# A copy of four norm factors to all partitions by GpSimd, placed behind the issue of the transfer that gathers the factors' row

## The chip, the cores and the metric

One core of one Trainium2 chip. The metric is the device time of one execution in microseconds (us), lower is better; the median of three runs is compared.

## What is computed

Two encoder layers over 512 tokens of width 1024, in float32. Each layer normalises x by its root mean square, sends it through one wide input projection, runs three attention branches (multi-head latent attention, a neighbourhood attention on a grid, a sliding-window attention), gates and sums them, projects and adds to x; then a second norm, an up projection of 2 x 2816 columns, a convolution of width 3 along the tokens, a gated GELU and a down projection. The part that matters here:

```python
def rmsnorm(x, g):
    y = xf * lax.rsqrt(jnp.mean(xf * xf, axis=-1, keepdims=True) + EPS)
    return (y * g.astype(jnp.float32)).astype(x.dtype)
...
h = rmsnorm(x, norm1_g[l])
...
q = (rmsnorm(c_q, g_qa) @ w_uq)
kv = (rmsnorm(c_kv, g_kva) @ w_ukv)
...
h = rmsnorm(x, norm2_g[l])
```

So each token has a factor 1/sqrt(mean square) for each of these norms, and each factor scales one column of the activations.

## The kernel before, in words

Activations lie transposed: 128 channels on the partitions, 512 tokens along a row, so x is eight tiles of 128x512. Every float32 matrix and activation is split into a high and a low part (`split`, lines 145 to 152: ScalarE casts the high part, VectorE subtracts to get the low part), and every product is three matmuls (lines 162 to 164). Weights come through a ring of three raw tiles, filled by transfers on SyncE's queue (line 114), and are split into `whi` and `wlo`, three pairs deep (lines 120 to 131).

The norm is applied after the product. `rs_tokens` (line 184) turns the sums of squares with four TensorE transposes, reduces them on VectorE (L193) and makes the factors on GpSimd: `ms` (L195, L196), then `rt` (L198, L200), a 128x4 tile that holds token 128j+p in row p, column j. `rs_spread` (line 203) brings the 512 factors to every partition: a transfer on GpSimd's queue writes `rt` as one row of one partition (`row`, L207), and GpSimd's partition_broadcast copies that row to all 128 partitions (L208), into `rb` or `rbk`. It runs six times, three times a layer:

- in `do_lat` (line 404), where the first norm's `rb` is made; the lines behind it, 416 and 417, make `r1` from `rt` with two GpSimd instructions, which `rs_q` and `rs_k` need at L195 and L200. In layer 0 `do_lat4` (lines 423 and 424) then issues two parameter transfers on GpSimd's queue, each behind a small GpSimd copy that holds it back until `rt` is there;
- in `do_rb_k` (line 470), where the kv latent's `rbk` is made, which `do_kn` (line 494) multiplies into the keys (`ev`, L155);
- at the up projection (line 869), where the second norm's `rb` is made, which `conv` (line 877) multiplies into the products (`u`, L155).

Readers of `rb` in the attention stage are the key rotation (`do_kr`, line 450) and the gates (line 687). The values V take `rtk` itself as a scale on ScalarE (line 467, `ynh`).

**Order.** TensorE and SyncE run in program order, written by hand in the lists of `schedule`. VectorE, ScalarE and GpSimd are ordered by the framework's planner when the program is built: it plays the program through with modelled times, and when an engine is free in that play, the engine takes, of the instructions whose inputs are there, the one that stands first in the program. Weight splits are put ahead in this ranking (`high_priority(offset=PRIO)`, line 129). The chip then runs each engine's list in exactly that order, and an instruction whose input is late holds up all that is listed behind it. GpSimd's library loads are put into the finished lists afterwards, wherever an instruction needs other library code than the one before: in the profile they are pairs of MODIFY_POOL_CONFIG. The broadcast needs one library, the tensor_tensor and tensor_scalar instructions of GpSimd (L195 to L200, L416, L417) another.

Of the kernel before, what the change touches and what calls it, by code (L numbers as in the profile page):

```python
# [10 lines left out]
F32 = mybir.dt.float32  # L11
# [6 lines left out]
P = 128  # L18
# [40 lines left out]
class Trunk:  # L59
# [143 lines left out]
    def rs_spread(self, rt, rb):  # L203


        row = self.const.tile([P, S], F32, tag="sq0", name="row")
        self.nc.gpsimd.dma_start(row[0:1, :], rt[:])  # L207
        self.nc.gpsimd.partition_broadcast(rb[:].rearrange("q (j p) -> q j p", p=P),  # L208
                                           row[0:1, :].rearrange("q (p j) -> q j p", p=P))

# [882 lines left out]
```

## Time and profile before

| | |
|---|---|
| median of three runs | 1702.35 us (1701.78 to 1702.51) |
| the profiled execution | 1702.94 us, its span 1701.2 us |
| TensorE busy | 1694.5 us, 100% of the span |
| VectorE, ScalarE, GpSimd busy | 1145.2, 867.4 and 53.1 us |
| broadcasts on GpSimd | 6, of 1.2 us each |

Times in the rows below are microseconds from the span's start; the second column is an instruction's length; in brackets stands how long its engine sat idle before it and what ended that ("issue": nothing that the profile shows as work, such as a library load). POOL is GpSimd, DVE is VectorE, ACT is ScalarE, PE is TensorE, PEld its weight loads. L numbers are lines of the kernel. What lies outside the span is 1.7 us.

### The profile page before, as it was taken

To read this page: it belongs to the slowest core of one execution; us is meant where nothing else is said; L and a number is where in the kernel's file an instruction comes from. 1 tells how busy PE (TensorE), PEld (TensorE's weight loads), DVE (VectorE), ACT (ScalarE), POOL (GpSimd) and SP (SyncE) were. 2 spreads that over 40 slices of the span, in tenths; PEclk is the share of its full clock that TensorE was granted. 3 is DMA by queue.
4 is the path that set the end of the run, shared out by engine and by line. 5 is a ranking of instruction groups with operands and counts; after the bars stand their busy time and mean duration, and the time that the engine had idled before them with its cause. 6 is when DMAs were issued, how large, how long until landed. Compare 5 with 4: busy or idle time off the path is not lost.

```text
span 1701.2 us, 21123 instructions
## 1 busy us (share of the span) xinstructions
PE 1694.5 (100%) x7924; PEld 1416.0 (83%) x7924; DVE 1145.2 (67%) x1872; ACT 867.4 (51%) x1504; POOL 53.1 (3%) x107
## 2 busy tenths in 40 slices
PE   9999999999999999999999999999999999999998
PEld 8888888888888888888888888888888888888887
DVE  7767885887558777734367678768766587777234
ACT  7665555775435444433256656557744444444232
POOL 1100000000000000000011100000000000000000
PEclk9999999999999999999999999999999999999999
DMA  5223233222324333323233232432223333333231
GB/s 178 80 83 84 82 93 87 75 69 75 106 81 118 99 100 99 96 87 103 81 96 81 81 84 69 107 85 69 63 81 107 98 112 99 94 93 98 87 105 69
DMA packets 289398, 155.38 MB, mean 91 GB/s; under 512 B 9008, under 2 KB 285248, under 8 KB 289296
## 3 DMA queue, kind: packets, MB, share of 16 engines
q1 hardware_dynamic: 286752, 148.92, 30.7%
q0 software_dynamic: 2256, 4.83, 1.0%
q8 instruction: 62, 1.02, 0.3%
q14 instruction: 40, 0.33, 0.1%
q10 hardware_dynamic: 288, 0.29, 0.0%
HBM read 151.89 MB, written 2.10 MB: 91 GB/s over the span
## 4 chain that ended last, share of the span: by engine, by line
PE 96%; DVE 0%; DMA 0%; issue 0%; ACT 0%; ACTq 0%
PE ps_d L162 21%; PE ps_d L164 21%; PE ps_d L163 21%; PE ps_g L164 7%; PE ps_g L162 7%; PE ps_g L163 7%; PE ps_tp L816 1%; PE ps_po L672 1%; PE ps_tp L526 1%; PE ps_tp L657 1%; PE ps_s L786 1%; PE ps_s L785 1%; PE ps_po L831 1%; PE ps_po L830 1%; PE ps_s L639 0%; PE ps_s L638 0%
## 5 line engine op out<-in xcount | busy, mean ns | idle before, releaser
L148 ACT CAST whi<-raw 128x1024 fp32r<-128x1024 f32 (+4 forms) x339 | 301.4, 889 | 572.6 <-PE ps_d L163 344.2
L162 PE MATMUL ps_d<-hh,whi 128*128 128x512 f32 x1328 | 518.6, 391 | 0.0
L164 PE MATMUL ps_d<-hh,wlo 128*128 128x512 f32 x1328 | 517.2, 389 | 0.0
L163 PE MATMUL ps_d<-hl,whi 128*128 128x512 f32 x1328 | 517.1, 389 | 0.0
L149 DVE TENSOR_TENSOR wlo<-raw,whi 128x1024 fp32r<-128x1024 f32 (+4 forms) x337 | 344.7, 1023 | 173.9 <-ACT whi L148 173.1
L164 PEld LDWEIGHTS ps_d<-hh,wlo 128*128 128x128 f32 x1328 | 249.2, 188 | 52.7 <-DVE wlo L149 0.5
L162 PEld LDWEIGHTS ps_d<-hh,whi 128*128 128x128 f32 x1328 | 249.3, 188 | 50.7 <-DVE rot L155 0.5
L163 PEld LDWEIGHTS ps_d<-hl,whi 128*128 128x128 f32 x1328 | 249.4, 188 | 50.1
L162 PE MATMUL ps_g<-ff,whi 128*128 128x512 f32 x334 | 129.9, 389 | 0.0
L163 PE MATMUL ps_g<-ff,whi 128*128 128x512 f32 x334 | 129.9, 389 | 0.0
L164 PE MATMUL ps_g<-ff,wlo 128*128 128x512 f32 x334 | 129.9, 389 | 0.0
L155 DVE TENSOR_TENSOR u<-ps_d,rb 128x512 f32<-128x512 f32 x80 | 55.3, 691 | 63.1 <-PE ps_d L164 63.1
L155 DVE TENSOR_TENSOR gz<-ps_d,rb 128x512 f32<-128x512 f32 x48 | 33.1, 690 | 82.0 <-PE ps_d L164 81.9
L880 ACT ACTIVATE c<-u,par 128x512 f32<-128x512 f32 x88 | 71.7, 815 | 16.4 <-DVE u L155 16.2
L163 PEld LDWEIGHTS ps_g<-ff,whi 128*128 128x128 f32 x334 | 62.7, 188 | 13.1
L162 PEld LDWEIGHTS ps_g<-ff,whi 128*128 128x128 f32 x334 | 62.7, 188 | 13.0
L164 PEld LDWEIGHTS ps_g<-ff,wlo 128*128 128x128 f32 x334 | 62.7, 188 | 13.0
L149 DVE TENSOR_TENSOR pl<-ps_tp,ph 128x512 fp32r<-128x512 f32 x104 | 68.4, 682 | 3.2 <-ACT ph L148 2.9
L886 ACT ACTIVATE c<-c 128x512 f32<-128x512 f32 x44 | 27.8, 632 | 80.5 <-DVE c L882 80.5
L882 DVE SCALAR_TENSOR_TENSOR c<-u,par,c 128x511 f32<-128x511 f32 x88 | 66.0, 750 | 2.8
L881 DVE SCALAR_TENSOR_TENSOR c<-u,par,c 128x511 f32<-128x511 f32 x88 | 65.5, 745 | 0.6 <-ACT c L880 0.6
L148 ACT CAST ph<-ps_tp 128x512 fp32r<-128x512 f32 x104 | 56.9, 585 | 3.6 <-PE ps_tp L526 2.8
(283 smaller groups left out, 2580.9 us busy)
## 6 DMA issues: line engine op xcount, KB each, us to landing
raw<-in_w_in_dram SPq DMA_DIRECT2D x86, 512.0 KB, 4.0
raw<-in_w_up_dram SPq DMA_DIRECT2D x80, 512.0 KB, 3.8
raw<-in_w_down_dram SPq DMA_DIRECT2D x32, 512.0 KB, 4.2
raw<-in_w_down_dram SPq DMA_DIRECT2D x16, 384.0 KB, 3.5
raw<-in_w_in_dram SPq DMA_DIRECT2D x18, 256.0 KB, 2.9
raw<-in_w_br_mla_dram SPq DMA_DIRECT2D x16, 256.0 KB, 2.7
raw<-in_w_br_na_dram SPq DMA_DIRECT2D x16, 256.0 KB, 2.7
raw<-in_w_br_gqa_dram SPq DMA_DIRECT2D x16, 256.0 KB, 2.7
```

What stands on the lines that cost most here:

```text
L148: nc.scalar.copy(hi, src)
L149: nc.vector.tensor_sub(lo, src, r32(hi))
L155: self.nc.vector.tensor_tensor(out, a, b, ALU.mult)
L162: mm(ps, sh, mh, start=first and k == 0, stop=False)
L163: mm(ps, sh, ml, start=False, stop=False)
L164: mm(ps, sl, mh, start=False, stop=last and k == n - 1)
L526: self.nc.tensor.transpose(tp[:, b * P:(b + 1) * P], self.pts[h, b][:, kc * P:(kc + 1) * P], self.idf)
L657: self.nc.tensor.transpose(tp[:, i * P:(i + 1) * P], self.pts["n", h, bp][:, i // 2, (i % 2) * P:(i % 2) * P + P], self.idf)
L880: nc.scalar.activation(c, u, AF.Identity, bias=pr[:, PC_CB + fi:PC_CB + fi + 1], scale=cw[:, 1:2])
L881: nc.vector.scalar_tensor_tensor(c[:, 1:], u[:, :S - 1], cw[:, 0:1], c[:, 1:], ALU.mult, ALU.add)
L882: nc.vector.scalar_tensor_tensor(c[:, :S - 1], u[:, 1:], cw[:, 2:3], c[:, :S - 1], ALU.mult, ALU.add)
L886: nc.scalar.activation(c, c, AF.Gelu_apprx_tanh)
```

## The change

`rs_spread` gets a tile `few` of 128x4 and, between the issue of the transfer and the broadcast of the row, a second partition_broadcast, which copies the first row of `rt` (four factors) to all partitions. Nothing reads `few`.

```diff
     def rs_spread(self, rt, rb):
         row = self.const.tile([P, S], F32, tag="sq0", name="row")
         self.nc.gpsimd.dma_start(row[0:1, :], rt[:])
+        few = self.small.tile([P, 4], F32, tag="few", name="few", bufs=1)
+        self.nc.gpsimd.partition_broadcast(few[:], rt[0:1, :])
         self.nc.gpsimd.partition_broadcast(rb[:].rearrange("q (j p) -> q j p", p=P),
                                            row[0:1, :].rearrange("q (p j) -> q j p", p=P))
```

## Rows read from the trace of the kernel before

**Rows 1.** The page, busy time of each engine: us (share), instructions.
```profile
PE 1694.5 (100%) x7924; PEld 1416.0 (83%) x7924; DVE 1145.2 (67%) x1872; ACT 867.4 (51%) x1504; POOL 53.1 (3%) x107
```
**Rows 2.** TensorE's timeline, the longest wait between two matmuls after the start.
```profile
68.69 0.39 PE L510 MATMUL ps_s<-kr,qr 128*128 128x512 f32 x1
69.34 0.50 PE L506 MATMUL ps_s<-kn,qn 128*128 128x512 f32 x1 [0.27 <-DVE pt L513]
```
**Rows 3.** Waits of TensorE's weight loads: us in total, times, longest.
```profile
PEld ps_d L164 <- DVE wlo L149: 0.5, 2, 0.3
```
**Rows 4.** Lines L208 and L207: library loads of the broadcasts; landing of the row.
```profile
L208 POOLq MODIFY_POOL_CONFIG  x12: 11/37/37, 30.4 to 1340.8; - x12
...
DMA to landing us min/median/max: 2.0/2.4/4.3
```
**Rows 5.** GpSimd's timeline, the first norm of layer 0 to its keys.
```profile
9.60 0.30 POOL masks.py:199 TENSOR_SCALAR_AFFINE_SELECT idf<-idf 128x128 f32<-128x128 f32 x1 [8.67 <-issue]
...
26.08 0.86 POOL L207 DMA_DIRECT2D row<-rt  x1 [0.31 <-POOL rt L198]
26.98 0.21 POOL L416 TENSOR_TENSOR r<-rt 128x4 f32<-128x4 f32 x1
...
37.16 1.25 POOL L208 PARTITION_BROADCAST rb<-row  x1 [6.99 <-issue]
45.21 0.87 POOL L195 TENSOR_TENSOR ms<-ms,r 128x4 f32<-128x4 f32 x1 [6.80 <-DVE acc L181]
...
47.60 0.57 POOL L200 TENSOR_TENSOR rt<-rt,r 128x4 f32<-128x4 f32 x1
51.07 0.58 POOL L195 TENSOR_TENSOR ms<-ms,r 128x4 f32<-128x4 f32 x1 [2.89 <-DVE ms L193]
...
53.97 0.43 POOL L200 TENSOR_TENSOR rt<-rt 128x4 f32<-128x4 f32 x1
54.69 0.74 POOL L207 DMA_DIRECT2D row<-rt  x1 [0.30 <-POOL rt L200]
61.41 1.21 POOL L208 PARTITION_BROADCAST rbk<-row  x1 [5.98 <-issue]
```
**Rows 6.** GpSimd's timeline, the first norm of layer 1.
```profile
857.43 0.74 POOL L207 DMA_DIRECT2D row<-rt  x1 [0.30 <-POOL rt L198]
...
858.65 0.26 POOL L417 TENSOR_SCALAR r<-rt 128x4 f32<-128x4 f32 x1
865.54 1.24 POOL L208 PARTITION_BROADCAST rb<-row  x1 [6.63 <-issue]
884.15 0.20 POOL L195 TENSOR_TENSOR ms<-ms,r 128x4 f32<-128x4 f32 x1 [17.38 <-DVE ms L193]
...
893.00 0.58 POOL L195 TENSOR_TENSOR ms<-ms,r 128x4 f32<-128x4 f32 x1 [6.13 <-DVE ms L193]
```
**Rows 7.** VectorE's timeline, the first reader of layer 1's rb.
```profile
888.64 0.68 DVE L155 TENSOR_TENSOR ev<-ev,rb 64x512 f32<-64x512 f32 x1
```
**Rows 8.** GpSimd's timeline, the broadcast for the up projection of layer 1.
```profile
1347.43 1.22 POOL L208 PARTITION_BROADCAST rb<-row  x1 [6.94 <-issue]
```
**Rows 9.** ScalarE and VectorE at the same place.
```profile
1344.93 0.62 ACT L148 CAST whi<-raw 128x512 fp32r<-128x512 f32 x1 [2.10 <-PE ps_g L163]
...
1348.68 0.69 DVE L155 TENSOR_TENSOR u<-ps_g,rb 128x512 f32<-128x512 f32 x1 [5.12 <-POOL rb L208]
...
1349.29 0.68 DVE L149 TENSOR_TENSOR wlo<-raw,whi 128x512 fp32r<-128x512 f32 x1
```
**Rows 10.** VectorE and ScalarE in layer 0: first readers of rb, rtk and rbk.
```profile
46.71 0.68 DVE L155 TENSOR_TENSOR ev<-ev,rb 64x512 f32<-64x512 f32 x1
...
54.43 0.69 ACT L151 ACTIVATE ynh<-ps_d,rt 128x512 fp32r<-128x512 f32 x1 [1.54 <-POOL rt L200]
...
62.65 0.69 DVE L155 TENSOR_TENSOR ev<-ps_d,rbk 128x512 f32<-128x512 f32 x1 [2.91 <-POOL rbk L208]
```
**Rows 11.** The windows view: stretch, length, then busy us (instructions) of PE, PEld, DVE, ACT, POOL; granted clock.
```profile
62.00:75.00 13.00, 12.73 (x57) 10.21 (x56) 9.37 (x22) 9.33 (x19) 0.62 (x1) 1.00 0.27 76
```

## The prediction

> **What bounds the kernel now.** First the page: TensorE is busy 1694.5 of 1701.2 us [rows 1], so a change on GpSimd, busy for 53.1 us, can only act through a wait of TensorE. Second, TensorE's timeline and waits, for how much it waits at all after the start. The longest gap is at 69.34, where a score product follows its predecessor's start (68.69) by 0.65 us instead of the 0.23 us of a steady stream, 0.42 us lost [rows 2]; the only other wait that hangs on this change is that of two products for a low weight part, 0.5 us together for the loads, about 0.1 us each for the products [rows 3]. So hardly 0.6 us can be won here. Third, GpSimd's timeline around the six broadcasts. Before each of them GpSimd sits idle for 5.98 to 6.99 us though the row has landed 2.0 to 4.3 us after its issue [rows 4 to 6, 8]: what fills the gap is the library load, a pair of MODIFY_POOL_CONFIG [rows 4] that starts behind the instruction before it, not behind the row's landing. The reader should see two things. The load already runs beside the transfer. And what comes after the load of layer 0 is tight: VectorE waits 2.91 us for `rbk` and ScalarE 1.54 us for the factors `rtk` [rows 10].
>
> **What the planner knows.** At the up projection VectorE's list has `u` ahead of a weight split `wlo`; `wlo` had its input at 1345.55 (ScalarE's cast ends), while `u` had to wait for `rb` until 1348.68 [rows 9]. Weight splits rank higher, so in the planner's play `u` must have been startable before that cast was done, some 3 us earlier than on the chip: the planner's GpSimd has no library load in it. Without the load `rb` would be there at about 1343.0: the issue ends at 1340.49 (6.94 ahead of the broadcast), the row lands 2.0 us after the start of a 0.74 us issue, so 1.3 later, and the broadcast takes 1.22 [rows 4 to 6, 8]. That fits.
>
> **The change part by part.** Nothing is removed or moved in the program's text. Added are six broadcasts of four elements, no transfer, no reader.
>
> *What one costs by itself.* The trace has no broadcast of four elements. From above it costs what one of 512 costs, 1.25 us [rows 5]; from below the 0.2 us of a four-element instruction on GpSimd [rows 5, 6]; it might even cost less than nothing if it takes a share of a first call's time off the broadcast behind it, but that one would have to get shorter by more than the new one is long, and I exclude that. I take 0.3 us, near the four-element rows, since the work is four elements.
>
> *Where it goes.* `few` needs `rt` alone, which is there before the transfer is issued, and it stands ahead of `r1` in the program; the row's broadcast has to wait for the landing. So in the play GpSimd takes the issue, then `few`, and then, while the row is still under way (landing 2.0 us after an issue of 0.74 us leaves 1.3 us, and `few` takes 0.3), the two `r1` instructions, as it takes them before the row's broadcast now [rows 5, 6]. At the two first norms the list then reads: issue, `few`, `r1`, `r1`, (in layer 0 the parameter copies and transfers), broadcast, `rs_q`. The library changes at each step: to the broadcast's, back, to the broadcast's, back. Two loads become four. At the other four places (`rbk` and the up projection of both layers) only the row's broadcast follows, in the same library: no further load.
>
> *Prices of a load.* To the broadcast's library 6.99 us at this place [rows 5], 5.98 to 6.94 elsewhere [rows 5, 6, 8]. Back: the only tight row is 6.80 us, but its end may be VectorE's, which is named as releaser [rows 5], so it is an upper bound there; from below I take the shortest load of the other kind, 5.98; from above the very first load of the kernel, 8.67 [rows 5]. I take 6.5.
>
> *Layer 0, step by step* [rows 5]. The issue ends at 26.94. Load 6.99: `few` at 33.9, done 34.2. Load back 6.5: `r1` at 40.7. From there to the end of the parameter issues as now, 26.98 to 30.17 (37.16 less 6.99), 3.2 us: 43.9. Load 6.99 and 1.25 for the row: `rb` at 52.2, 13.8 later than 38.41. Load back 6.5: `rs_q` starts at 58.7, lasts 45.21 to 48.17, 3.0: 61.6. `rs_k` (51.07 to 54.40, 3.3) follows at once, as its inputs are there: `rtk` at 65.0, 10.6 later than 54.40. Then 0.3 and the issue 0.74, load 5.98, `few` 0.3, broadcast 1.21: `rbk` at 73.5, **10.9 us later** than 62.62. What queues behind: VectorE stands at 46.71 until `rb` is there, 5.5 us, which holds the next weight splits; ScalarE stands at 54.43 until `rtk` is there, with the casts of the next weights behind it, so TensorE runs out of weights at about 62; VectorE then stands at 62.65 for `rbk` [rows 10]. The last of these decides, since the score products need the keys, and the present gap at 69.34 [rows 2] hangs on the same chain: all of the 10.9 us shows on TensorE. With 5.98 for every load the term is 7.9; with 8.67 for the loads back and 1.25 for `few`, 17.1.
>
> The Trainium skill (GPSIMD Engine Reference, Instruction dispatch) has a freshly loaded library cost about 6 us, measured as 5.95. By that price for all five loads the term would be an estimated 7.7 in place of 10.9, and the time about 1712. This trace's rows are longer in four of six cases (the two places not shown read 6.92 and 5.98), so I stay with them.
>
> *Layer 1, first norm* [rows 6, 7]. The issue ends at 858.17; 6.63, 0.3, 6.5, 0.7 (`r1`), 6.63 and 1.24 put `rb` at 880.2, before its first reader at 888.64. Load back: `rs_q` at 886.7 instead of 884.15, done before `rs_k` at 893.00. Cover: 8 us for `rb`, and the long way to the first scores for `rs_q`. Cost nothing.
>
> *The other three places.* `rbk` of layer 1 and both `rb` of the up projection come 0.3 us later. VectorE waits for each already [rows 9], and the two low weight parts of [rows 3] are listed behind `u`: 0.6 us for both up projections. For `rbk` of layer 1 TensorE has no gap now, so between 0 and 0.3; I take 0.1. With 1.25 for `few` these would be 3.7.
>
> *TensorE's clock.* It is at 1.00, the 2.4 GHz level, throughout [rows 11], and no wait here is long enough to show what one of 8 us does. If it falls to the lower level the products that follow take twice 0.23 us. From below 0; from above the six products of the second head's keys and the twenty of the first scores, 5.9 us. I take the six, 1.4 us: they are the first behind the last wait, and what ran slowly before that wait is paid in it. The Trainium skill (TensorE: Matmul & The Clock Gate, the clock gate) has a long idle TensorE drop to 1.2 GHz and come back after some work; no run here shows it.
>
> **The sum.** 10.9 + 0.6 + 0.1 + 1.4 = 13.0 us. On the profiled execution 1702.94 + 13.0 = 1715.9; that execution stood 0.6 us above the median, so 1715.3 against 1702.35. A measurement of this kernel can tell about 0.2%, 3.4 us, from no change.
>
> **The rivals.** *One: the two broadcasts stay together at every place* (the planner holds `r1` back, or puts `few` behind it). The place is the first norm, the price the two loads, and what decides is whether in the play the row lands before `r1` is taken. Then no load is added, the row's broadcast comes 0.3 us later, and only the small terms are left: 0.6 + 0.1 + 0.3 for layer 0's `rbk`, 1703.4; with 1.25 for `few` 1707. For it: where nothing else is ready, GpSimd goes straight on to the broadcast [rows 8]. Against it: `r1` is taken ahead of the row in both layers now. Chance 0.19. *Two: the change does nothing*, because nobody reads `few` and it is dropped, or because it lies wholly inside a load's shadow: 1702.35. Chance 0.04. *Three: it helps.* If `few` and row together run ahead of the parameter issues, layer 0's `rb` comes at 35.4 instead of 38.4, but its reader starts at 46.71 [rows 10]; if a second call is much shorter than 1.2 us, the waits of VectorE shrink. All waits together give 0.6 us: 1701.7, within the measurement. Chance 0.02 with a gain that could be told.
>
> **How the numbers follow.** The forecast, loads doubled at the first norms, 0.75: 1715.3, with its own range 1710.5 (loads at 5.98, clock unmoved, little for `few`) to 1719 (a quarter of the upper extras, which are 6.2, 3.0 and 4.5 us). The range must reach down to the first rival to leave out no more than 2 in 10: 1702.6 to 1719. Slower by over 0.2%: 0.75 and a small part of the first rival, 0.78. Same: 0.20. Faster: 0.02.
>
> **What would show it.** Right: GpSimd's timeline with four idle stretches of 6 to 7 us between 27 and 59, `rb` at about 52, `rbk` at about 73, TensorE waiting some 8 us near 62 and 3 us near 72, MODIFY_POOL_CONFIG in more pairs, a granted clock under 1.00 near 75. Layer 1 shows the same loads and no gap on TensorE. Wrong: `few` and the row's broadcast side by side at 27 to 38, and TensorE's timeline unchanged.

## The result and the profile after

The changed kernel takes 1710.44 us (median of five runs, 1710.27 to 1711.02) against 1702.35 us: the ratio is 1.0046, with a 95% interval from 1.0035 to 1.0057, so it is slower by 8.1 us. One of the five runs of the kernel before took 7416 us, which does not move its median. Its profiled execution took 1710.27 us with a span of 1708.4 us, 7.2 us more than the one of before. The difference between 8.1 and 7.2 lies in the start of the two executions: the one of before issued its first row at 26.08 [rows 5], this one at 25.09, and TensorE's loads of its first weights are 1.0 us earlier too from their third group on (7.62 before, 6.61 after). From that issue to the end it is 1675.1 us before and 1683.3 after, 8.2 us more, close to the 8.1 us between the medians. Among the executions profiled below the issue lies between 25.05 and 26.03.

TensorE's work is the same, 7924 matmuls; VectorE's and ScalarE's lists hold the same instructions in the same order as before. The page, busy time of each engine:

```profile
PE 1696.4 (99%) x7924; PEld 1416.1 (83%) x7924; DVE 1145.0 (67%) x1872; ACT 867.3 (51%) x1504; POOL 52.0 (3%) x113
```

What answers to [rows 5] is GpSimd's timeline in layer 0:

```profile
25.09 0.86 POOL L208 DMA_DIRECT2D row<-rt  x1 [0.31 <-POOL rt L198]
32.01 0.28 POOL L210 PARTITION_BROADCAST few<-rt  x1 [6.05 <-issue]
39.63 0.63 POOL L419 TENSOR_TENSOR r<-rt 128x4 f32<-128x4 f32 x1 [7.34 <-issue]
...
41.31 1.29 POOL L427 DMA_DIRECT2D par<-in_par_dram  x2 [0.17 <-POOL par L426]
48.69 1.21 POOL L211 PARTITION_BROADCAST rb<-row  x1 [6.09 <-issue]
56.96 0.66 POOL L195 TENSOR_TENSOR ms<-ms,r 128x4 f32<-128x4 f32 x1 [7.06 <-DVE qn L149]
...
59.30 0.20 POOL L195 TENSOR_TENSOR ms<-ms,r 128x4 f32<-128x4 f32 x1
...
59.86 1.01 POOL L198 TENSOR_TENSOR rt<-ms,cst 128x4 f32<-128x4 f32 x1
60.95 0.20 POOL L200 TENSOR_TENSOR rt<-rt 128x4 f32<-128x4 f32 x1
61.45 0.74 POOL L208 DMA_DIRECT2D row<-rt  x1 [0.30 <-POOL rt L200]
68.10 0.28 POOL L210 PARTITION_BROADCAST few<-rt  x1 [5.91 <-issue]
68.27 1.22 POOL L211 PARTITION_BROADCAST rbk<-row  x1
```

Read it by the brackets: four idle stretches of 6.05 to 7.34 us, between the issue and the copy, the copy and `r1`, the parameter issues and the row, the row and `rs_q`. Before there were two. At `rbk` copy and row stand side by side, one load ahead of both. The views of the lines L210, L419, L211 and L195 show where the load instructions are, two to a load:

```profile
L210 POOLq MODIFY_POOL_CONFIG  x12: 37/37/37, 26.2 to 1347.9; - x12
...
L419 POOLq MODIFY_POOL_CONFIG  x4: 108/108/108, 32.2 to 872.1; - x4
...
L211 POOLq MODIFY_POOL_CONFIG  x4: 11/24/37, 42.8 to 880.3; - x4
...
L195 POOLq MODIFY_POOL_CONFIG  x4: 129/129/129, 49.8 to 887.4; - x4
```

The loads of L419 and L211 are new: two in each layer, at the first norm. All six copies have a load of their own, but at the other four places it is the one that the row's broadcast had before. In layer 1 GpSimd's timeline has the same four stretches (compare [rows 6]):

```profile
864.45 0.74 POOL L208 DMA_DIRECT2D row<-rt  x1 [0.30 <-POOL rt L198]
871.84 0.28 POOL L210 PARTITION_BROADCAST few<-rt  x1 [6.64 <-issue]
879.41 0.19 POOL L419 TENSOR_TENSOR r<-rt 128x4 f32<-128x4 f32 x1 [7.29 <-issue]
...
886.16 1.24 POOL L211 PARTITION_BROADCAST rb<-row  x1 [6.20 <-issue]
894.37 0.69 POOL L195 TENSOR_TENSOR ms<-ms,r 128x4 f32<-128x4 f32 x1 [6.98 <-DVE acc L181]
...
900.05 0.58 POOL L195 TENSOR_TENSOR ms<-ms,r 128x4 f32<-128x4 f32 x1 [2.89 <-DVE ms L193]
```

The last of these rows tells why they cost nothing there: `rs_k` waits for VectorE, 2.89 us, and not for GpSimd.

In layer 0 the delay passes from engine to engine. VectorE and ScalarE after, the answers to [rows 10] and the instructions that TensorE then waits for:

```profile
49.93 0.68 DVE L155 TENSOR_TENSOR ev<-ev,rb 64x512 f32<-64x512 f32 x1 [4.11 <-POOL rb L211]
56.16 0.68 DVE L149 TENSOR_TENSOR qn<-ps_d,qn 128x512 fp32r<-128x512 f32 x1
61.19 0.69 ACT L151 ACTIVATE ynh<-ps_d,rt 128x512 fp32r<-128x512 f32 x1 [5.08 <-POOL rt L200]
64.48 0.50 ACT L148 CAST whi<-raw 128x384 fp32r<-128x384 f32 x1
64.62 0.75 DVE L152 SCALAR_TENSOR_TENSOR ynl<-ps_d,rt,ynh 128x512 fp32r<-128x512 f32 x1 [0.60 <-ACT ynh L151]
69.53 0.69 DVE L155 TENSOR_TENSOR ev<-ps_d,rbk 128x512 f32<-128x512 f32 x1 [3.03 <-POOL rbk L211]
```

And TensorE's waits over the whole span (us in total, times, longest), of which before had only the score wait of 0.3 us beside the start:

```profile
PE ps_d L162 <- DVE ynl L152: 2.9, 1, 2.9
...
PE ps_d L162 <- DVE qn L149: 1.0, 1, 1.0
PE ps_s L509 <- DVE pt L516: 1.0, 1, 1.0
PE ps_d L164 <- DVE wlo L149: 0.7, 1, 0.7
```

Four waits, 5.6 us, all between 55 and 77 us. The first, 2.9 us at 65.52, ends with VectorE's `ynl`, the low part of the third product of V. By the kernel's turns of PSUM banks (the places into which TensorE writes its products; `banks` in `do_mla_open` and `do_mla_attn`) the queries of the second head go into the bank of that product, and the bank is free when `ynl` has read it, at 64.62 + 0.75 = 65.37. The weight part that they need was cast earlier, by 64.48 + 0.50 = 64.98. The wait at 56.89 is of the same kind: the gates' product takes the bank that VectorE's `qn` has read at 56.16 + 0.68 = 56.84, and `qn` stands in VectorE's list behind the 4.11 us for `rb`. Most of the rest of the loss is pace. TensorE's timeline:

```profile
62.24 0.39 PE L164 MATMUL ps_d<-hh,wlo 128*128 128x512 f32 x1
65.52 0.47 PE L162 MATMUL ps_d<-mg,whi 128*128 128x512 f32 x1 [2.89 <-DVE ynl L152]
...
66.62 0.63 PE L162 MATMUL ps_d<-mg,whi 128*128 128x512 f32 x1
67.05 0.63 PE L163 MATMUL ps_d<-mg,whi 128*128 128x512 f32 x1
...
70.61 0.51 PE L164 MATMUL ps_d<-mg,wlo 128*128 128x512 f32 x1 [0.74 <-DVE wlo L149]
```

Behind the wait the products start 0.43 us apart, about twice the 0.23 of before it. The windows view has the granted clock at 0.50, the 1.2 GHz level, from 66.2 to 68.7, and at 0.89 over the longer stretch (the value before the last two), against 1.00 in [rows 11]:

```profile
66.20:68.70 2.50, 2.50 (x7) 1.97 (x6) 0.30 (x1) 0.00 (x0) 0.60 (x2) 0.50 0.26 79
62.00:77.00 15.00, 10.40 (x36) 7.48 (x35) 10.35 (x18) 8.70 (x16) 1.58 (x3) 0.89 0.17 46
```

Which of these delays decides, the traces say by one number. GpSimd starts the second norm of layer 0, which follows TensorE's whole attention stage, at 495.78 before and at 502.69 after:

```profile
495.78 0.56 POOL L196 TENSOR_SCALAR ms<-ms 128x4 f32<-128x4 f32 x1 [252.51 <-DVE ms L193]
...
502.69 0.56 POOL L196 TENSOR_SCALAR ms<-ms 128x4 f32<-128x4 f32 x1 [252.53 <-DVE ms L193]
```

Counted from the end of `rbk`'s broadcast (62.62 before, 69.49 after) that is 433.2 us in both, and between 433.1 and 433.4 us in all twelve traces of this document, although `rbk` is there between 36.5 and 45.0 us after the row's issue. So in layer 0 the time goes by `rbk`, and the waits above are only how its delay is dealt out: in another execution of the changed kernel (the one under "The copy as two halves") TensorE's waits in the same stretch are 0.6, 2.6 and 2.7 us, and none at the scores. From the second norm of layer 0 to the end it is 1205.4 us before and 1205.7 after.

### The profile page after: what moved, and what is told of

Read it like the earlier page. It is cut to its first block, busy times and chain, and to the rows that moved or that the text cites. A ratio compares the mean times of both kernels' runs of the same rounds, so it can differ in the third digit from the quotient of the medians.

```text
span 1708.4 us, 21137 instructions
## 1 busy us (share of the span) xinstructions
PE 1696.4 (99%) x7924; PEld 1416.1 (83%) x7924; DVE 1145.0 (67%) x1872; ACT 867.3 (51%) x1504; POOL 52.0 (3%) x113
## 4 chain that ended last, share of the span: by engine, by line
PE 95%; DVE 0%; DMA 0%; issue 0%; POOL 0%; ACT 0%; ACTq 0%
PE ps_d L162 21%; PE ps_d L164 21%; PE ps_d L163 21%; PE ps_g L164 7%; PE ps_g L163 7%; PE ps_g L162 7%; PE ps_tp L819 1%; PE ps_po L675 1%; PE ps_tp L529 1%; PE ps_tp L660 1%; PE ps_s L789 1%; PE ps_s L788 1%; PE ps_po L834 1%; PE ps_po L833 1%; PE ps_s L642 0%; PE ps_s L641 0%
## 5 line engine op out<-in xcount | busy, mean ns | idle before, releaser
L148 ACT CAST ph<-ps_tp 128x512 fp32r<-128x512 f32 x104 | 56.9, 585 | 3.6 <-PE ps_tp L529 2.8
```

The lines of the kernel that those rows point to most:

```text
L148: nc.scalar.copy(hi, src)
```

## The experiments

The theory was that the two added loads in front of layer 0's keys make the whole loss, because the copy stands ahead of `r1` in GpSimd's list and the two need different libraries. Each kernel is the changed one with the edit shown, five rounds beside the kernel before, which read 1702.74 to 1702.97 us in these sets. Ratios are to that kernel, with their 95% interval.

### The copy at the first norm of layer 0 alone

```diff
-        few = self.small.tile([P, 4], F32, tag="few", name="few", bufs=1)
-        self.nc.gpsimd.partition_broadcast(few[:], rt[0:1, :])
+        if self.item == "lat" and self.l == 0:
+            few = self.small.tile([P, 4], F32, tag="few", name="few", bufs=1)
+            self.nc.gpsimd.partition_broadcast(few[:], rt[0:1, :])
```

> The copy of four factors is kept at the first norm of layer 0 alone. Theory (the two added library loads in front of layer 0's keys are the whole loss): 7.6 to 8.1 us over the kernel before, some 1710.2 us, with rbk about 6.9 us later in the trace and the same pairs of waits on TensorE between 55 and 77 us. Rival (each of the six copies costs a share): a sixth of the loss, about 1703.7. Rival (the planner arranged other engines anew because of the copies): somewhere between, and a different order of VectorE's list.

1709.78 us, 7.0 over the kernel before (1.0042, 1.0029 to 1.0054), so one copy of six brings most of the loss; equal shares are excluded. It fell a little short of the expected 7.6, by less than the interval's width. VectorE's list stands in the order of before, which excludes the second rival. `rbk`, counted from the row's issue, comes 7.0 us later than before; TensorE's waits there are 0.5, 2.6 and 2.3 us, without the one at the scores. GpSimd's timeline of this kernel:

```profile
67.94 1.20 POOL L212 PARTITION_BROADCAST rbk<-row  x1 [6.09 <-issue]
```

### The copy at the first norm of layer 1 alone

The same edit with `self.l == 1`.

> The copy is kept at the first norm of layer 1 alone, where it also doubles the loads. Theory (the cover of 8 us before the first reader of rb, and of the values' factors, takes the loads in): no change, 1702.2 to 1702.8, although rb comes about 13 us later. Rival (a doubled load costs what it costs in layer 0): about 1710.

1702.93 us (1.0001, 0.9992 to 1.0009): no change, with the two added loads in place, as GpSimd's timeline shows:

```profile
864.41 0.28 POOL L211 PARTITION_BROADCAST few<-rt  x1 [6.55 <-issue]
871.56 0.34 POOL L420 TENSOR_TENSOR r<-rt 128x4 f32<-128x4 f32 x1 [6.87 <-issue]
...
878.58 1.24 POOL L212 PARTITION_BROADCAST rb<-row  x1 [6.32 <-issue]
```

A load is not dear as such; what it costs is decided by who waits behind it.

### The copy at the four other places

The same edit with `if self.item != "lat"`.

> The copy is left out at both first norms and kept at the other four places, where it stands directly ahead of the row's broadcast in the same library. Theory: the broadcast starts 0.17 us later at each (the pitch of the copy in the changed kernel), of which 0.1 to 0.4 us in all reaches the end, 1702.5 to 1702.8. Rival (equal shares): two thirds of the loss, about 1707.7.

1703.72 us (1.0005, 0.9996 to 1.0014): 1.0 us over the median of before, a little above what was expected, and within the measurement no change. Two thirds of the loss are excluded. The three partial kernels add up to the loss of all six copies: 7.0 + 0.2 + 1.0 = 8.2 us, though each of the three is known to no better than 1.5 to 2 us.

### All copies, r1 made ahead of the spread

```diff
         hooks.setdefault(early[0], []).append(self.norm_sums)
+        hooks[early[0]].append(self.make_r1)
...
-        self.r1 = self.small.tile([P, 8], F32, tag="r1", name="r1")
-        self.nc.gpsimd.tensor_tensor(self.r1[:, 0:4], self.rt, self.rt, ALU.mult)
-        self.nc.gpsimd.tensor_scalar(self.r1[:, 4:8], self.rt, -MLA_SCALE, None, ALU.mult)
```

(`make_r1` holds the three lines that are taken out.)

> All six copies stay; r1 is made ahead of the spread in the program. Theory (order of the library's users, not the copies): GpSimd's list goes r1, r1, issue, copy, broadcast, with one load ahead of the copy and one behind the broadcast, and the loss is gone: 1702.4 to 1703.2. In layer 0 the parameter copies and issues may stand between the copy and the broadcast, which needs no load. Rival (the copy's own cost): 1710 as in the changed kernel.

1703.68 us (1.0006, 0.9997 to 1.0015): with all six copies in place, the loss is gone but for 0.9 us that the measurement cannot tell from nothing. GpSimd's timeline shows what order does. There is one load, and the copy, the parameter copies and issues and the row run on it:

```profile
25.14 0.20 POOL L422 TENSOR_TENSOR r<-rt 128x4 f32<-128x4 f32 x1
...
33.12 0.28 POOL L210 PARTITION_BROADCAST few<-rt  x1 [6.22 <-issue]
33.26 0.40 POOL L429 COPY par<-rt 128x4 f32<-128x4 f32 x2
...
35.16 1.26 POOL L211 PARTITION_BROADCAST rb<-row  x1
```

### All copies, r1 on VectorE

```diff
-        self.nc.gpsimd.tensor_tensor(self.r1[:, 0:4], self.rt, self.rt, ALU.mult)
-        self.nc.gpsimd.tensor_scalar(self.r1[:, 4:8], self.rt, -MLA_SCALE, None, ALU.mult)
+        self.nc.vector.tensor_tensor(self.r1[:, 0:4], self.rt, self.rt, ALU.mult)
+        self.nc.vector.tensor_scalar(self.r1[:, 4:8], self.rt, -MLA_SCALE, None, ALU.mult)
```

> All six copies stay; the two instructions of r1 run on VectorE. Theory: nothing between the copy and the row's broadcast needs the other library, two loads instead of four at each first norm, 1702.4 to 1703.2; a little of VectorE's time (two instructions under 0.2 us and their wait for the factors) may show. Rival (the copies cost by themselves): 1710.

1702.97 us (1.0000, 0.9992 to 1.0009). A second way of taking the other library's users from between the two broadcasts takes the loss away too. It does not beat the kernel before either; no run here pointed to a version that does.

### A small instruction of the loaded library in place of the copy

```diff
-        self.nc.gpsimd.partition_broadcast(few[:], rt[0:1, :])
+        self.nc.gpsimd.tensor_scalar(few[:], rt[:], 2.0, None, ALU.mult)
```

> In place of the six copies stand six tensor_scalar instructions of 128x4 on GpSimd, which use the library that is loaded already (the tile holds twice the factors instead of a copy of four; nothing reads it). Theory: an instruction of 0.2 us in front of a load that runs anyway, 1702.4 to 1703.0, loads as before the change. Rival (one more GpSimd instruction behind the issue is what hurts, whatever its library): 1710.

1703.71 us (1.0004, 0.9995 to 1.0013). Six more instructions at the same place in the program, of 0.27 to 0.41 us, without a change of library: 0.8 us over the kernel before, a little above what was expected and within the measurement no change; no 8 us.

### Each copy twice

```diff
         self.nc.gpsimd.partition_broadcast(few[:], rt[0:1, :])
+        self.nc.gpsimd.partition_broadcast(few[:], rt[0:1, :])
```

> Each copy of four factors stands twice in a row. Theory (the load is paid by the change of library, not by the number of broadcasts): 0.17 us more at each place, of which the end sees 0.2 to 0.6 us, about 1710.7 to 1711.1. Rival (every broadcast brings its own cost): the loss doubles, about 1718.

1712.82 us (1.0058, 1.0045 to 1.0071). The loss does not double, so broadcasts do not cost by their number; but the 2 us over the changed kernel are more than the 0.6 that was allowed. GpSimd's timeline at the first up projection shows one reason: the second copy writes the same tile and starts 0.37 us behind the first, not 0.17, so the row comes 0.53 us after the first copy. Against the 0.17 us of the changed kernel that is 0.36 us more at each of the four places without `r1`, at most 1.4 us together; the rest is not traced. At the two first norms the planner put the second copy behind `r1`, next to the row, where it needs no load of its own.

```profile
513.06 0.28 POOL L210 PARTITION_BROADCAST few<-rt  x1 [6.78 <-issue]
513.43 0.26 POOL L211 PARTITION_BROADCAST few<-rt  x1
513.59 1.21 POOL L212 PARTITION_BROADCAST rb<-row  x1
```

### The copy as two halves

To tell the number of broadcasts from the wait between them, two broadcasts of two factors each, into different columns.

```diff
-        self.nc.gpsimd.partition_broadcast(few[:], rt[0:1, :])
+        self.nc.gpsimd.partition_broadcast(few[:, 0:2], rt[0:1, 0:2])
+        self.nc.gpsimd.partition_broadcast(few[:, 2:4], rt[0:1, 2:4])
```

> The copy of four factors is made as two broadcasts of two factors each, into two halves of the tile, so that the second need not wait for the first. Theory (a further broadcast in the loaded library costs its pitch, about 0.15 us at each of the four tight places): 0.3 to 0.7 us over the changed kernel run beside it. Rival (every further broadcast costs half a us a place, as in the kernel with the doubled copy): 2 us over it.

> The changed kernel itself, once more on this chip, as the measure for the kernel with two halves: 8 us over the kernel before, about 1710.6.

The halves take 1711.91 us (1.0054, 1.0041 to 1.0067), the changed kernel beside them 1710.76 (1.0046, 1.0032 to 1.0060). The second half starts 0.16 us behind the first and the row 0.15 behind that:

```profile
512.62 0.26 POOL L210 PARTITION_BROADCAST few<-rt  x1 [6.83 <-issue]
512.78 0.26 POOL L211 PARTITION_BROADCAST few<-rt  x1
512.93 1.21 POOL L212 PARTITION_BROADCAST rb<-row  x1
```

The medians differ by 1.15 us, between the two expectations, and the intervals overlap; the changed kernel's own five runs here spread over 2.4 us. This part is inconclusive: a further broadcast in the loaded library costs tenths of a microsecond in the trace, and how much of it the end sees is below what these runs resolve.

### TensorE kept busy in its wait

```diff
     def do_qn(self, h):
+        if self.l == 0 and h == 1:
+            idle = self.psum.tile([P, S], F32, tag="b7", name="idle")
+            for _ in range(13):
+                self.nc.tensor.matmul(idle, self.h[0][0][:, 0:P], self.h[0][0], start=True, stop=True)
```

> The changed kernel with 13 products of 128x512 put into TensorE's list ahead of the second head's queries of layer 0, into a bank that nothing reads; they fill the wait of 2.9 us behind which the products ran at half pace. Theory (the slow products are paid inside the wait for the next low weight part, so the clock costs nothing): the granted clock stays at 1.00 and the time at 1710.2 to 1710.8. Rival (the fall of the clock is part of the loss): 1 to 1.5 us less, about 1709.2.

1710.58 us (1.0045, 1.0033 to 1.0058), the time of the changed kernel; the interval alone would not exclude the rival's 1 us. The trace decides. The windows view has the clock at 1.00 in the stretch where it was 0.89, and TensorE's wait for the low weight part has grown by what the products gained: 0.7 us in the changed kernel, it is now 2.4 us, the longest of the two in this line:

```profile
62.00:77.00 15.00, 11.67 (x51) 8.93 (x50) 10.29 (x21) 8.22 (x16) 1.38 (x2) 1.00 0.20 52
```

```profile
PE ps_d L164 <- DVE wlo L149: 2.9, 2, 2.4
```

From the end of `rbk`'s broadcast to the second norm of layer 0 it is 433.2 us, as with the slow clock. So the slow clock cost nothing where it fell on the queries: the product behind the slow ones waits for a low weight part that stands behind `rbk`'s first reader in VectorE's list anyway.

## Why the prediction was right, and where its size was off

**The direction and the mechanism held.** The list came out as forecast, issue, `few`, `r1`, parameter issues, row, with four loads at both first norms and one at the other places. Layer 0 pays (7.0 us alone), layer 1 does not (0.2), the other four places show 1.0, which the measurement cannot tell from nothing. That the whole delay of `rbk` shows on TensorE, as forecast, is what the constant 433 us say. The first rival, the two broadcasts side by side, is what the four other places and the two kernels with `r1` moved show: 1703.0 to 1703.7, close to the 1703.4 worked out for it. That the planner's play has no load in it was argued from [rows 9] and fits the list it made: a GpSimd that counted 6 to 7 us a load would have had the row landed long before `few` was done, and would not have gone back to `r1`.

**The time was 5 us too high** (1715.3 against 1710.4). The range from 1702.6 to 1719 held it only because it was stretched down to the first rival: the forecast's own range began at 1710.5, just above what was measured. (Two of its sums are off by a tenth: with 5.98 for every load the term is 7.8 and not 7.9, and the third rival's `rb` would come at 35.5 and not 35.4.) The terms against the trace, each from the row's issue on:

| term | forecast | measured |
|---|---|---|
| five loads up to `rbk` (6.99, 6.5, 6.99, 6.5, 5.98) | 33.0 | 32.5 (6.05, 7.34, 6.09, 7.06, 5.91) |
| `r1` to the end of the parameter issues | 3.2 | 3.0 |
| `rs_q` and `rs_k` | 6.3 | 4.2 (56.96 to 61.15) |
| two copies of four | 0.6 | 0.45 (0.28 long at the first norm; at `rbk` the row starts 0.17 behind it) |
| `rbk` later by | 10.9 | 7.9 |
| the copies at the up projections and layer 1's `rbk` | 0.7 | 0.3 (7.20 at the end less 6.91 at layer 0's second norm) |
| clock | 1.4 | 0 |

The step that was mis-sized most is "`rs_q` lasts 3.0, `rs_k` 3.3": these durations were taken from [rows 5], and in that trace `rs_k`'s three cheap steps took 0.58, 0.19 and 0.43 us and its power step 1.87:

```profile
52.01 1.87 POOL L198 TENSOR_TENSOR rt<-ms,cst 128x4 f32<-128x4 f32 x1
```

In the changed kernel they take 0.20, 0.20, 0.20 and 1.01. VectorE stands still from 57.6 to 61.9 there, waiting for these very factors, while it was splitting weights before; in layer 1, with VectorE at work, the power step takes 1.88 again. That GpSimd is faster when VectorE rests fits, but was only read off and not tried, and it is not the whole rule: in the trace of before, `rs_q`'s power step took 1.06 us (46.46 to 47.52) while VectorE worked on `ev` [rows 10]. What can be said is that a price taken beside a busy engine need not hold for the moment in which that engine waits.

The load back to the other library was taken as 6.5 between 5.98 and 8.67. In this trace it is longer, 7.34 and 7.29 where nothing else holds `r1` (6.65 and 7.17 in another execution of the changed kernel), and the load to the broadcast's was shorter at this place than before, 6.05 for 6.99; that the two errors cancel to half a microsecond is luck. The Trainium skill's price (GPSIMD Engine Reference, Instruction dispatch), 5.95 a load, gave an estimated term of 7.7 and a time of about 1712, nearer than mine, though not for its reason: in this trace the loads to the broadcast's library come near it (6.05, 6.09 and 5.91), the loads back do not (7.34 and 7.06), and the nearness comes from `rs_q` and `rs_k`.

The clock term failed in its place, not in its cause: the clock fell as feared, to 0.50, behind a gap of 3.3 us between the starts of two products (62.24 and 65.52). The Trainium skill (TensorE: Matmul & The Clock Gate, Part 1: The HAM clock gate) has an idle TensorE fall to 1.2 GHz; the trace agrees. But the slow products were the second head's queries, and these lie ahead of the wait at 70.61. I had charged the products behind the last wait; in this trace the clock was back at 1.00 by then. In two other traces, of the kernel with the copy at layer 0's first norm alone and of the other execution of the changed kernel, it fell where I had put it, behind the wait at 70.25 and 71.90; the windows view of the second:

```profile
72.00:75.00 3.00, 3.00 (x7) 2.38 (x8) 2.74 (x4) 2.59 (x5) 0.00 (x0) 0.50 0.15 44
```

There too it did not cost the 1.4 us: from the end of `rbk`'s broadcast to the second norm of layer 0 these two took 433.4 and 433.3 us instead of 433.2, and the score wait of 1.0 us at 76.22 is not there. The slow products ran in the time of that wait.

**The other points.** VectorE did stand for `rb` (4.11 us for the 5.5 forecast), ScalarE for `rtk` (5.08), VectorE for `rbk` (3.03). TensorE's waits near 62 and 72 were forecast at 8 and 3 us; they measured 2.9 and 0.7, with 1.0 us each at 56.9 and 76.2, and the half pace between. TensorE did not run out of weights at 62, as forecast: it waited for the bank of the third product of V, which came free 0.4 us after the weight part was cast. Both hang on `rtk`, so the forecast's path through ScalarE and VectorE stands.

## What to carry to other kernels

GpSimd's instructions come from different libraries, and a change of library costs 5.8 to 7.8 us on its queue in these traces (8.3 once, in the kernel with the small instruction; the first load of all, in the kernel before, 8.67 [rows 5]); an instruction that is put between users of one library is priced by the loads that it adds, not by its 0.28 us. A load starts when the queue reaches it (the pair of L210 at 26.2, the issue having ended at 25.95) and runs beside a transfer anyway, so a small instruction put there to bring it forward gains nothing where the load already stood behind the issue. Where a planner orders an engine without knowing of such loads, look at the list it made, and keep the users of one library together by their place in the program or by their engine.

## What was not expected of the hardware

A load back to the arithmetic library ahead of `r1`, where nothing else is awaited, took 6.65 to 7.8 us in the kernels with the copy at that place. In each of them that was more than the load to the broadcast's library just before it took, 5.8 to 6.6 us, once by no more than 0.05 us (6.65 against 6.60). Why is not known. A broadcast of four words takes 0.28 us and lets the next one start 0.17 us after its own start, against 1.21 us for 512. GpSimd's four-element copy runs on either library: in the kernel with `r1` first it stands between two broadcasts with no load around it, and in the kernel before it stands behind `r1` (28.50), likewise with none.
